# A hybrid decoder layer on one core: a new hand order for TensorE's mixer work

## The chip, the core and the metric

The kernel runs on one core of a Trainium2 chip. A core has five engines with an instruction queue each: TensorE (PE in the profile; its weight loads are listed as PEld), VectorE (DVE), ScalarE (ACT), GpSimd (POOL) and SyncE (SP), which here only starts transfers. The metric is the device time of one execution in microseconds; less is better.

## What is computed

One layer of a decoder, for 1024 prompt tokens and 8 sequences of 8 new tokens each, 1088 tokens in all, in 32-bit floats:

```python
x = x + 0.5 * rms(swiglu(rms(x) @ w_up1) @ w_down1)
h = rms(x); z = h @ w_in                  # q,k,v | qkv of B | z | a,b | gates
oA = sliding_window_attention(q, k, v)    # window 128, 8 heads, 2 kv heads, a sink per head
q, k, v = silu(conv4(qkv))                # short causal convolution, branch B
oB = gated_delta_rule(l2(q), l2(k), v, decay, beta)   # 4 heads, chunks, state 128x128
oB = rms(oB) * silu(z)
m = sigmoid(gA) * (oA @ w_a) + sigmoid(gB) * (oB @ w_b)
x = x + rms(m @ w_out)
x = x + 0.5 * rms(swiglu(rms(x) @ w_up2) @ w_down2)
```

Caches and states for the next call are outputs too.

## The kernel before

Features lie on the partitions and tokens along the free axis, in three chunks `CH` of 384, 384 and 320 tokens (the last holds 256 prompt tokens and the 64 new ones). The three stages follow each other: feed-forward 1, the mixers, feed-forward 2. A projection of the mixers is cut into units of 128 output features. `gemm` (L142 to L144) multiplies in three products for each of 8 slices of the input features: high part by high part, high by low part of the activations, low part of the weights by high. One slice of one chunk, so three products, is called a **k-step** here. Weights arrive raw, ScalarE copies out the high part (L115) and VectorE subtracts it for the low part (L116).

In the mixers the program order of TensorE is the order in which the code is written (`manual_schedule`). The other engines' orders are the scheduler's, by priorities; each engine then runs its rows strictly in that order. Between the small products of the attention and of the delta rule the code calls `fill(us)`: it takes k-steps from the front of `queue`, a list of generators, until their planned costs (0.54 us for 384 tokens, 0.46 us for 320) reach the number given. The queue's units are

- `z_unit` and `gate_unit`: the projections for z and for the gates gA and gB, 24 k-steps each. A gate's result needs little of VectorE: ScalarE's tanh, and one L672 on VectorE in the last chunk;
- `conv_unit`: a projection of branch B, followed on VectorE by three multiply-adds (L865) and by L893 a chunk, with a tail for the new tokens in the last chunk (L875, L885 to L890).

The attention runs over 16 items. `att_s` makes the scores (L954), VectorE adds the mask (L965) and does the softmax (L815 to L818, L822 to L824), and one item later `att_t` transposes what L824 wrote (L983); `att_v` (L999) is one more item behind. A fill stands after each item.

The delta rule takes the heads in two pairs. For a pair, `first` makes the products of keys and queries (L1192, read by VectorE's L1195, and L1202, read by L1205), `invert` solves 32x32 triangles on VectorE over a transfer out and back, with one long fill for TensorE meanwhile, and `second` (from L1255 on) combines the blocks, runs the decode over 8 chunks (L1315, L1323, L1333, L1342, L1343), multiplies the state of the new tokens (L1355: 16 columns a product), and ends with the norm products (L1395). `together(a, b)` alternates two heads at each `yield`; a yield's two numbers are the fill after the first head's piece and after the second's. The results of these products use two PSUM tiles `ph` and two `py`; the queue's units use three tiles `pa`, and the heads share one tile `po` for L1333.

What is left of the queue after the second pair is done by `finish`, then come the last two gates, and then `br`, the branch products, whose inputs are loaded (L1505) and split (L195 on ScalarE, L196 on VectorE) from what the mixers wrote to memory.

Of the kernel before, what the change touches and what calls it, by code (L numbers as in the profile page):

```python
# [13 lines left out]
P = 128  # L14
# [21 lines left out]
def body(ctx: ExitStack, tc: tile.TileContext, d):  # L36
# [769 lines left out]
    def st():  # L806
        return s2b.tile([P, 20], F32, tag="st", name=uid("st"), bufs=4)
# [27 lines left out]
    def fill(us):  # L835
        while us > 0 and queue:
# [3 lines left out]
            else:  # L840
                us -= t

    def finish(units):
        for u in units:
            if u in queue:
                queue.remove(u)
                drain(u)
# [100 lines left out]
    def att_s(it):  # L948
        n, tp2 = items[it]
        k0 = 128 if n == 0 else 0  # L950
        ps = (ph(), py())
        for j in range(2):
            for g2, hs in enumerate(half2):
                mm = nc.tensor.matmul(  # L954
                    ps[g2][:, j * 256 + k0 : j * 256 + 256],
                    YA[tp2 * 2 + j][hs, n * P : n * P + P],
                    kT[hs, (n - 1) * P + k0 : (n + 1) * P],
                    start=True,
                    stop=True,
                )  # L960
                if masked:
                    tc.add_manual_dep(mm.ins, masked[-1], SYNC, reason="both halves start together")
        s4 = sbs[it % 2][:, :1024].rearrange("p (h k) -> p h k", k=256)[:, :, k0:256]
        for g2 in range(2):
            mask = nc.vector.tensor_tensor(  # L965
                out=s4[:, 2 * g2 : 2 * g2 + 2, :],
                in0=ps[g2].rearrange("p (j k) -> p j k", k=256)[:, :, k0:256],
                in1=cst[:, C_AM + k0 : C_AM + 256].unsqueeze(1).to_broadcast([P, 2, 256 - k0]),
                op=ALU.add,
            )  # L970
        masked.append(mask.ins.name)
        softmax(s4, vec[:, V_SK + 4 * tp2 : V_SK + 4 * tp2 + 4], st())

    def att_t(it):
        n, tp2 = items[it]
# [35 lines left out]
    def attention_prompt():  # L1011
        n = len(items)
        for it in range(n + 2):
            if it < n:
                att_s(it)
            if it >= 2:
                att_v(it - 2)
            if 1 <= it <= n:
                att_t(it - 1)
            fill(7.5 if it == 0 else 8.5 if it == n - 1 else 4.8)  # L1020
        for t in range(4):
            nc.sync.dma_start(oad[t, :, :NPR], YA[t][:, :NPR])

# [78 lines left out]
    class Head:  # L1102
# [140 lines left out]
        def second(self, pks):  # L1243
# [75 lines left out]
            for c in range(8):  # L1319
                w, cs, ix = chunk_of(c, h)  # L1320
                p = ps[c]
                if c > 0:
                    nc.tensor.matmul(p[:, 0:128], M[:, cs], S, start=False, stop=True)  # L1323
                vns = ar[:, c % 2, :]
                nc.vector.tensor_scalar_mul(vns, p[:, 0:128], tk["kds"][:, ix : ix + 1])
                vn = ar[:, 2 + c % 2, :]
                nc.scalar.copy(vn, p[:, 0:128])
                yield 0.0, 0.0
                if c < 7:
                    uv(c + 1)  # L1330
                yield 0.0, 0.4
                pk = pks()[:, 128 * (h % 2) : 128 * (h % 2) + 128]
                nc.tensor.matmul(pk, k[:, cs], vns, start=True, stop=True)  # L1333
                S2 = ar[:, 4 + c % 2, :]
                if c > 0:
                    nc.vector.scalar_tensor_tensor(
                        out=S2, in0=S, scalar=tk["gtot"][:, ix : ix + 1], in1=pk, op0=ALU.mult, op1=ALU.add
                    )
                else:
                    nc.vector.tensor_copy(S2, pk)  # L1340
                if c > 0:
                    nc.tensor.matmul(p[:, 256:384], S, q[:, cs], start=True, stop=False)  # L1342
                nc.tensor.matmul(p[:, 256:384], vn, QK[:, cs], start=c == 0, stop=True)  # L1343
                nc.scalar.copy(QK[:, cs], p[:, 256:384])
                S = S2
                yield 0.0, 0.0
            nc.sync.dma_start(d["dpo"][h], S)

            ss = slice(NPR, NT)
# [3 lines left out]
            mqv = mq.rearrange("p (g b t) -> p b g t", g=2, t=8)  # L1353
            for b in range(8):
                nc.tensor.matmul(pv[:, b], S0[:, b, :], mqv[:, b], start=b == 0, stop=False)  # L1355
            nc.tensor.matmul(p[:, 0:64], v8, U[:NSM, ss], start=False, stop=True)
            vnT = ar[:, 0, 0:64]
            nc.scalar.copy(ar[:, 0, :], p[:, 0:128])
# [29 lines left out]
                    out=L[:, 512 * hf : 512 * hf + 512], in0=L[:, 512 * hf : 512 * hf + 512], in1=p6, op=ALU.add  # L1388
                )
            nc.sync.dma_start(d["dso"][:, h].rearrange("b p e -> p b e"), S0)  # L1390
            yield 0.0, 5.0
            for a, b in CH:
                cs = slice(a, b)
                pq = pb()
# [9 lines left out]
    def together(a, b):  # L1404

        for us in a:
            fill(us[0])
            fill(next(b)[1])

    def invert(heads):  # L1410

        a, b = heads
        Md, Ld = (t[:68, :NPR].rearrange("p (r s) -> p r s", s=32) for t in (a.A[7], b.A[7]))
        tt = a.R2
        for i, x in enumerate(heads):
            nc.sync.dma_start(Md[34 * i : 34 * i + 34], bm[x.h])
        nc.vector.memset(Ld, 0.0)
        nc.vector.memset(b.A[7][:68, 0:1024:33], 1.0)
        for j in range(31):
            m = 31 - j  # L1420
            tv = tt[:68, : m * (j + 1)].rearrange("p (a b) -> p a b", b=j + 1)
            nc.vector.tensor_tensor(
                out=tv,
                in0=Md[:, j + 1 :, j : j + 1].to_broadcast([68, m, j + 1]),
                in1=Ld[:, j : j + 1, 0 : j + 1].to_broadcast([68, m, j + 1]),
                op=ALU.mult,
            )
            nc.vector.tensor_tensor(out=Ld[:, j + 1 :, 0 : j + 1], in0=Ld[:, j + 1 :, 0 : j + 1], in1=tv, op=ALU.subtract)
        nc.vector.tensor_copy(Md, Ld.rearrange("p r s -> p s r"))
        for i, x in enumerate(heads):  # L1430
            h, L, U = x.h, x.A[1], x.A[5]
            nc.sync.dma_start(blocks32(ud[h]), Md[34 * i : 34 * i + 32])
            nc.sync.dma_start(bu[h][32:34], Md[34 * i + 32 : 34 * i + 34])
            nc.sync.dma_start(blocks32(ld[h]), Ld[34 * i : 34 * i + 32])
            nc.sync.dma_start(U[:, :NPR].rearrange("p (c s) -> p c s", s=P), whole_rows(ud[h]))
            nc.sync.dma_start(L[:, :NPR].rearrange("p (c s) -> p c s", s=P), whole_rows(ld[h]))
            for b2 in range(2):
                nc.sync.dma_start(U[32 * b2 : 32 * b2 + 32, NPR + 32 * b2 : NPR + 32 * b2 + 32], bu[h][32 + b2])
        fill(51.0)

    heads = [Head(h, (HA, YA)[h % 2]) for h in range(4)]
    zs = [z_unit(h) for h in range(4)]
    gates = [gate_unit(i) for i in range(14)]
    with tc.manual_schedule(engines={mybir.EngineType.PE}):
        queue += zs[0:2] + gates[0:3] + heads[0].conv
        fill(2.0)
        values()
        attention_prompt()
# [3 lines left out]
        for hs in (heads[0:2], heads[2:4]):  # L1452
# [10 lines left out]
            else:  # L1463
# [7 lines left out]
                b.keys()  # L1471
                drain(b.conv[2])
                queue += zs[2:4] + gates[10:14]
            together(a.first(), b.first())
            invert(hs)
            state = []
# [211 lines left out]
```

## Time and profile before

| | before |
|---|---|
| median of 3 runs | 2410.01 us (2409.04 to 2410.94) |
| profiled execution | 2409.66 us |
| its span | 2407.7 us |
| mean granted TensorE clock | 0.990 |
| TensorE busy | 2354.6 us, 98% |
| VectorE busy | 1698.4 us, 71% |
| ScalarE busy | 1111.5 us, 46% |

The span runs from the first to the last instruction; 1.96 us of the profiled execution lie around it. A granted clock of 1.00 is 2.4 GHz, 0.50 is 1.2 GHz. "Busy" counts the time in which an instruction of the engine was running, at whichever clock.

### The profile page before, as it was taken

To read this page: it belongs to the slowest core of one execution; us is meant where nothing else is said; L and a number is where in the kernel's file an instruction comes from. 1 tells how busy PE (TensorE), PEld (TensorE's weight loads), DVE (VectorE), ACT (ScalarE), POOL (GpSimd) and SP (SyncE) were. 2 spreads that over 40 slices of the span, in tenths; PEclk is the share of its full clock that TensorE was granted. 3 is DMA by queue.
4 is the path that set the end of the run, shared out by engine and by line. 5 is a ranking of instruction groups with operands and counts; after the bars stand their busy time and mean duration, and the time that the engine had idled before them with its cause. 6 is when DMAs were issued, how large, how long until landed. Compare 5 with 4: busy or idle time off the path is not lost. (4 is left out here: it accounts for less than half of the span.)

```text
span 2407.7 us, 38879 instructions
## 1 busy us (share of the span) xinstructions
PE 2354.6 (98%) x14535; PEld 2295.2 (95%) x14535; DVE 1698.4 (71%) x3453; ACT 1111.5 (46%) x2314; POOL 22.1 (1%) x21
## 2 busy tenths in 40 slices
PE   8999999999999999999999999999999999999997
PEld 8999999999998988899898989999999999999997
DVE  8887667667688667675497457588976567676677
ACT  7644424323365455552563453366644433333344
POOL 0000000000000000000000000000000000000000
PEclk9999999999999999999999999999999999999998
DMA  7332212212453521314322346456433222122453
GB/s 274 120 121 86 67 51 84 71 58 91 167 191 130 181 69 48 126 45 125 105 98 70 99 153 203 131 195 221 134 104 94 67 62 79 62 71 84 158 168 130
DMA packets 173828, 276.19 MB, mean 115 GB/s; under 512 B 35276, under 2 KB 76208, under 8 KB 173632
## 3 DMA queue, kind: packets, MB, share of 16 engines
q1 hardware_dynamic: 173640, 273.71, 35.5%
q8 instruction: 114, 1.87, 0.3%
q14 instruction: 74, 0.61, 0.1%
HBM read 231.22 MB, written 43.41 MB: 114 GB/s over the span
## 5 line engine op out<-in xcount | busy, mean ns | idle before, releaser
L466 PE MATMUL pa<-ch,h_c_s 128*128 128x384 f32 x704 | 236.6, 336 | 3.1 <-DVE t L472 2.6
L468 PE MATMUL pa<-ch,l_c_s 128*128 128x384 f32 x704 | 235.6, 335 | 0.0
L467 PE MATMUL pa<-cl,h_c_s 128*128 128x384 f32 x704 | 235.5, 334 | 0.0
L472 DVE TENSOR_TENSOR t<-pa,t 128x384 f32<-128x384 f32 x308 | 170.6, 555 | 87.1 <-PE pa L468 87.0
L466 PE MATMUL pa<-ch,h_c_a 128*128 128x384 f32 x528 | 177.1, 335 | 0.0
L468 PE MATMUL pa<-ch,l_c_a 128*128 128x384 f32 x528 | 176.9, 335 | 0.0
L467 PE MATMUL pa<-cl,h_c_a 128*128 128x384 f32 x528 | 176.8, 335 | 0.0
L115 ACT CAST h_c_a<-r_c_a 128x512 fp32r<-128x512 f32 x132 | 81.8, 620 | 128.9 <-PE pa L467 111.9
L466 PEld LDWEIGHTS pa<-ch,h_c_s 128*128 128x128 f32 x704 | 132.2, 188 | 6.4 <-DVE t L472 6.3
L467 PEld LDWEIGHTS pa<-cl,h_c_s 128*128 128x128 f32 x704 | 132.2, 188 | 0.0
L468 PEld LDWEIGHTS pa<-ch,l_c_s 128*128 128x128 f32 x704 | 132.2, 188 | 0.0
L115 ACT CAST h_c_s<-q_c_s 128x512 fp32r<-128x512 f32 x132 | 82.0, 622 | 105.6 <-PE pa L467 92.4
L142 PE MATMUL pa<-xbh,h_ga 128*128 128x384 f32 (+1 forms) x384 | 130.8, 341 | 0.0
L144 PE MATMUL pa<-xbh,l_ga 128*128 128x384 f32 (+1 forms) x384 | 127.0, 331 | 0.0
L143 PE MATMUL pa<-xbl,h_ga 128*128 128x384 f32 (+1 forms) x384 | 127.0, 331 | 0.0
L466 PEld LDWEIGHTS pa<-ch,h_c_a 128*128 128x128 f32 x528 | 99.2, 188 | 0.4 <-ACT t L384 0.2
L468 PEld LDWEIGHTS pa<-ch,l_c_a 128*128 128x128 f32 x528 | 99.2, 188 | 0.0
L467 PEld LDWEIGHTS pa<-cl,h_c_a 128*128 128x128 f32 x528 | 99.2, 188 | 0.0
L115 ACT CAST h_c_s<-r_c_s 128x512 fp32r<-128x512 f32 x44 | 27.4, 622 | 149.5 <-PE pa L467 120.4
L142 PE MATMUL pa<-xbh,h_qkv 128*128 128x384 f32 (+1 forms) x288 | 95.5, 332 | 0.0
L144 PE MATMUL pa<-xbh,l_qkv 128*128 128x384 f32 (+1 forms) x288 | 94.3, 327 | 0.0
L143 PE MATMUL pa<-xbl,h_qkv 128*128 128x384 f32 (+1 forms) x288 | 94.2, 327 | 0.0
(627 smaller groups left out, 7277.8 us busy)
## 6 DMA issues: line engine op xcount, KB each, us to landing
r_c_a<-in_up_dram SPq DMA_DIRECT2D x132, 256.0 KB
r_wo<-in_wo_dram SPq DMA_DIRECT2D x48, 256.0 KB
q_c_a<-in_up_dram SPq DMA_DIRECT2D x44, 256.0 KB
q_ub<-in_up_dram SPq DMA_DIRECT2D x44, 256.0 KB
r_ub<-in_up_dram SPq DMA_DIRECT2D x44, 256.0 KB
r_ua<-in_up_dram SPq DMA_DIRECT2D x42, 256.0 KB
q_ua<-in_up_dram SPq DMA_DIRECT2D x42, 256.0 KB
r_da<-in_dn_dram SPq DMA_DIRECT2D x40, 256.0 KB
```

The costliest lines, as they stand in the source:

```text
L115: nc.scalar.copy(hi, full)
L142: nc.tensor.matmul(ps[:, :n], hi[:, j, :], at(xh, k), start=first, stop=False)
L143: nc.tensor.matmul(ps[:, :n], hi[:, j, :], at(xl, k), start=False, stop=False)
L144: mm = nc.tensor.matmul(ps[:, :n], lo[:, j, :], at(xh, k), start=False, stop=last)
L466: nc.tensor.matmul(ps, wh[:, k, :], xh[:, k, :], start=k == 0, stop=False)
L467: nc.tensor.matmul(ps, wh[:, k, :], xl[:, k, :], start=False, stop=False)
L468: nc.tensor.matmul(ps, wl[:, k, :], xh[:, k, :], start=False, stop=k == 3)
L472: nc.vector.tensor_tensor(out=out, in0=ps, in1=other, op=ALU.add)
```

## The change

It writes TensorE's work in the mixers in another order and gives some of VectorE's rows another priority. No product is added or taken away.

1. `turns` alternates the first head's three convolutions with the first three gates, chunk by chunk. Before, the three gates came first and the convolutions behind them.
2. The mask and the softmax of an attention item get a higher priority on VectorE and ScalarE.
3. The fill after the last attention item grows from 8.5 to 9.5.
4. A fill of 5.0 stands ahead of `first`.
5. `invert`'s fill grows from 51.0 to 53.5 for the second pair.
6. In the decode the k-step after the second head's L1315 (one each of the 8 chunks) goes; in the odd chunks one stands between the two heads' L1333 instead.
7. The 8 pairs of L1355's products are cut in two halves, with a k-step after each head's first half.
8. The fill ahead of the norm products shrinks from 5.0 to 2.0 for the first pair.

```diff
+    def turns(us, vs):
+
+        for pair_ in zip(us, vs):
+            for _ in CH:
+                for u in pair_:
+                    for _ in range(KT):
+                        yield next(u)
+            for u in pair_:
+                drain(u)
+
...
-        for g2 in range(2):
-            mask = nc.vector.tensor_tensor(
...
-        masked.append(mask.ins.name)
-        softmax(s4, vec[:, V_SK + 4 * tp2 : V_SK + 4 * tp2 + 4], st())
+        with tc.high_priority(offset=10000):
+            for g2 in range(2):
+                mask = nc.vector.tensor_tensor(
...
+            masked.append(mask.ins.name)
+            softmax(s4, vec[:, V_SK + 4 * tp2 : V_SK + 4 * tp2 + 4], st())
...
-            fill(7.5 if it == 0 else 8.5 if it == n - 1 else 4.8)
+            fill(7.5 if it == 0 else 9.5 if it == n - 1 else 4.8)
...
                 if c < 7:
                     uv(c + 1)
-                yield 0.0, 0.4
+                yield 0.0, 0.0
                 pk = pks()[:, 128 * (h % 2) : 128 * (h % 2) + 128]
                 nc.tensor.matmul(pk, k[:, cs], vns, start=True, stop=True)
...
                 S = S2
-                yield 0.0, 0.0
+                yield 0.4 * (c % 2), 0.0
...
             for b in range(8):
                 nc.tensor.matmul(pv[:, b], S0[:, b, :], mqv[:, b], start=b == 0, stop=False)
+                if b == 3:
+                    yield 0.4, 0.4
...
-            yield 0.0, 5.0
+            yield 0.0, 5.0 if h > 1 else 2.0
...
-        fill(51.0)
+        fill(51.0 if a.h == 0 else 53.5)
...
-        queue += zs[0:2] + gates[0:3] + heads[0].conv
+        queue += zs[0:2] + [turns(heads[0].conv, gates[0:3])]
...
+            fill(5.0)
             together(a.first(), b.first())
```

Lines of the changed kernel stand some 10 to 14 lines further down, so L824 keeps its number, but L954 becomes L964, L1192 becomes L1203, L1355 becomes L1366 and so on.

VectorE's order around the tail of the first convolution (`t` are the convolution's buffers, `s` the scores, `st` the softmax's small vectors, `pa` the PSUM tiles of the queue's units). Before:

```order
L885 TENSOR_SCALAR t_851_10310<-t_850_10306,vec 128x64
L865 SCALAR_TENSOR_TENSOR t_851_10310<-t_850_10306,vec,t_851_10310 128x256
L887 TENSOR_SCALAR t_852_10315<-t_850_10306,vec 128x64
L889 COPY sn_10318<-ncv 128x3
L890 COPY sn_10318<-t_850_10306 128x24
L888 TENSOR_TENSOR t_851_10310<-t_851_10310,t_852_10315 128x64
L965 TENSOR_TENSOR s_8347<-ph_10355,cst 128x512
L822 TENSOR_TENSOR st_10236<-st_10236 128x4
L887 TENSOR_SCALAR t_852_10315<-t_850_10306,vec 128x64
L823 RECIPROCAL st_10236<-st_10236 128x4
L965 TENSOR_TENSOR s_8347<-py_10356,cst 128x512
L824 TENSOR_TENSOR s_8355<-s_8355,st_10236 128x1024
```

and of the change, at the first convolution's tail:

```order
L898 TENSOR_TENSOR t_811_9913<-t_811_9913,t_812_9918 128x64
L897 TENSOR_SCALAR t_812_9918<-t_810_9909,vec 128x64
L898 TENSOR_TENSOR t_811_9913<-t_811_9913,t_812_9918 128x64
L897 TENSOR_SCALAR t_812_9918<-t_810_9909,vec 128x64
L116 TENSOR_TENSOR l_ga_0_10452<-r_ga_0_10449,h_ga_0_10451 128x512
L822 TENSOR_TENSOR st_9845<-st_9845 128x4
L898 TENSOR_TENSOR t_811_9913<-t_811_9913,t_812_9918 128x64
L823 RECIPROCAL st_9845<-st_9845 128x4
L875 SCALAR_TENSOR_TENSOR t_811_9913<-t_810_9909,vec,t_811_9913 128x256
L672 SCALAR_TENSOR_TENSOR t_815_9936<-pa_9884,r_8287 128x320
L116 TENSOR_TENSOR l_ga_1_10458<-r_ga_1_10455,h_ga_1_10457 128x512
L824 TENSOR_TENSOR s_8347<-s_8347,st_9845 128x1024
```

The next item's mask (L965) no longer stands ahead of L824 there; a gate's L672, which needs the gate's finished tile `pa_9884`, and one weight split L116 now do.

TensorE's order at the start of the first pair's `first` (`qkv` and `ga` are weights of a convolution and of a gate; `eye` is the identity for transposes). Before:

```order
L142 MATMUL pa_11466<-xbh_1_8284,h_qkv_1_11388 128x320
L143 MATMUL pa_11466<-xbl_1_8286,h_qkv_1_11388 128x320
L144 MATMUL pa_11466<-xbh_1_8284,l_qkv_1_11389 128x320
L1192 MATMUL ph_11520<-s_8348,s_8349 128x128 x4
L1194 MATMUL py_11521<-eye_72,s_8355 128x128 x4
L1192 MATMUL ph_11534<-s_8342,s_8343 128x128 x4
L1194 MATMUL py_11535<-eye_72,s_8347 128x128 x4
L1192 MATMUL ph_11546<-s_8348,s_8349 128x128 x4
```

and of the change:

```order
L142 MATMUL pa_11533<-xbh_1_8284,h_ga_1_10909 128x320
L143 MATMUL pa_11533<-xbl_1_8286,h_ga_1_10909 128x320
L144 MATMUL pa_11533<-xbh_1_8284,l_ga_1_10910 128x320
L1203 MATMUL ph_11557<-s_8348,s_8349 128x128 x4
L1205 MATMUL py_11558<-eye_72,s_8355 128x128 x4
L1203 MATMUL ph_11571<-s_8342,s_8343 128x128 x4
L1205 MATMUL py_11572<-eye_72,s_8347 128x128 x4
L1203 MATMUL ph_11583<-s_8348,s_8349 128x128 x4
```

The last convolution's k-steps no longer stand right ahead of the products: 11 k-steps of a gate do (4 of 384 tokens, 7 of 320). For the second pair there are 10 k-steps of z, of 384 tokens.

TensorE's order from the last decode chunk to the state products (head a writes `ph`, head b `py`). Before:

```order
L142 MATMUL pa_12402<-xbh_1_7322,h_ga_1_12398 128x384
L143 MATMUL pa_12402<-xbl_1_7324,h_ga_1_12398 128x384
L144 MATMUL pa_12402<-xbh_1_7322,l_ga_1_12399 128x384
L1333 MATMUL po_12546<-s_8355,s_8352 128x128
L1342 MATMUL ph_12519<-s_8348,s_8355 128x128
L1343 MATMUL ph_12519<-s_8354,s_8355 128x128
L1333 MATMUL po_12546<-s_8347,s_8340 128x128
L1342 MATMUL py_12521<-s_8342,s_8347 128x128
L1343 MATMUL py_12521<-s_8346,s_8347 128x128
L1355 MATMUL ph_12558<-mq_10996,s_8349 128x2x8 x8
L1356 MATMUL ph_12558<-s_8353,v_10998 128x64
```

and of the change:

```order
L1354 MATMUL ph_12544<-s_8354,s_8355 128x128
L142 MATMUL pa_12367<-xbh_1_7900,h_ga_1_12193 128x384
L143 MATMUL pa_12367<-xbl_1_7902,h_ga_1_12193 128x384
L144 MATMUL pa_12367<-xbh_1_7900,l_ga_1_12194 128x384
L1344 MATMUL po_12565<-s_8347,s_8340 128x128
L1353 MATMUL py_12546<-s_8342,s_8347 128x128
L1354 MATMUL py_12546<-s_8346,s_8347 128x128
L1366 MATMUL ph_12580<-mq_10996,s_8349 128x2x8 x4
L142 MATMUL pa_12367<-xbh_1_7900,h_ga_1_12193 128x384
L143 MATMUL pa_12367<-xbl_1_7902,h_ga_1_12193 128x384
L144 MATMUL pa_12367<-xbh_1_7900,l_ga_1_12194 128x384
L1366 MATMUL py_12589<-mq_11017,s_8343 128x2x8 x4
```

In this odd chunk the k-step has moved from ahead of head a's products to between the two heads' products, and a new one stands inside the state products. In even chunks there is none.

## Rows read from the trace of the kernel before

**Rows 1.** The page's first part: busy time of each engine, share of the span.

```profile
PE 2354.6 (98%) x14535; PEld 2295.2 (95%) x14535; DVE 1698.4 (71%) x3453; ACT 1111.5 (46%) x2314; POOL 22.1 (1%) x21
```

**Rows 2.** Waits of TensorE, 840 to 1460 us: us in total, times, longest.

```profile
PE ph L1192 <- DVE s L1195: 8.2, 2, 4.5
PE ph L983 <- DVE t L888: 3.1, 1, 3.1
PE ph L1255 <- DMA s<-ud: 2.1, 1, 2.1
PE pa L142 <- DVE t L1518: 1.4, 1, 1.4
...
PE po L1333 <- DVE s L1340: 0.5, 2, 0.3
```

**Rows 3.** Windows: length, busy time of each engine, TensorE's granted clock, DMA share, GB/s.

```profile
966.00:972.00 6.00, 4.42 (x21) 4.45 (x22) 3.78 (x11) 3.03 (x11) 0.00 (x0) 0.72 0.00 0
1065.00:1074.00 9.00, 7.09 (x38) 7.10 (x39) 7.56 (x22) 2.81 (x5) 0.00 (x0) 0.62 0.02 4
1181.00:1187.00 6.00, 6.00 (x27) 5.47 (x27) 3.00 (x6) 0.74 (x3) 1.90 (x1) 0.72 0.48 166
1277.00:1286.00 9.00, 6.10 (x35) 6.10 (x36) 8.22 (x22) 3.33 (x6) 0.00 (x0) 0.62 0.22 62
1392.00:1402.00 10.00, 10.00 (x52) 9.62 (x52) 2.82 (x7) 2.06 (x6) 3.79 (x2) 0.66 0.47 139
1406.00:1412.00 6.00, 5.44 (x19) 4.45 (x19) 2.43 (x5) 0.47 (x1) 0.00 (x0) 0.72 0.62 175
1156.00:1176.00 20.00, 20.00 (x151) 18.71 (x151) 9.06 (x28) 8.72 (x31) 0.00 (x0) 1.00 0.23 75
```

**Rows 4.** VectorE's timeline, 958 to 968: start, us, line and operation.

```profile
961.64 0.42 DVE L672 SCALAR_TENSOR_TENSOR t<-pa,r 128x256 f32<-128x256 f32 x1
961.98 0.68 DVE L116 TENSOR_TENSOR l_ga<-r_ga,h_ga 128x512 fp32r<-128x512 f32 x1
...
966.22 1.22 DVE L824 TENSOR_TENSOR s<-s,st 128x1024 f32<-128x1024 f32 x1
```

**Rows 5.** TensorE's timeline, 962 to 969.

```profile
962.29 0.48 PE L954 MATMUL ph<-s,s 64*128 64x256 f32 x1
...
963.35 1.08 PE L999 MATMUL po<-s,s 128*64 128x256 f32 x8
```

**Rows 6.** VectorE's timeline, 1061 to 1083.

```profile
1066.16 0.69 DVE L1195 TENSOR_TENSOR s<-ph,s 128x512 f32<-128x512 f32 x1
...
1071.58 0.69 DVE L1195 TENSOR_TENSOR s<-ph,R 128x512 f32<-128x512 f32 x1 [0.70 <-PE ph L1192]
...
1073.60 1.13 DVE L1205 SCALAR_TENSOR_TENSOR s<-ph,nk,s 128x128 f32<-128x128 f32 x4 [0.74 <-PE ph L1202]
```

**Rows 7.** TensorE's timeline, 1060 to 1082.

```profile
1060.32 1.05 PE L1192 MATMUL ph<-s,s 128*128 128x128 f32 x8
...
1080.67 0.42 PE L142 MATMUL pa<-xbh,h_ga 128*128 128x384 f32 x1
```

**Rows 8.** TensorE's timeline in the decode, one chunk from L1342 on.

```profile
1157.32 0.39 PE L1342 MATMUL ph<-s,s 128*128 128x128 f32 x2
1157.54 0.39 PE L1343 MATMUL ph<-s,s 128*128 128x128 f32 x2
1157.92 0.49 PE L1333 MATMUL po<-s,s 128*128 128x128 f32 x2
...
1160.98 0.49 PE L1333 MATMUL po<-s,s 128*128 128x128 f32 x2
```

**Rows 9.** TensorE's timeline: the last chunk of the last gates, then the branch products.

```profile
1441.19 0.31 PE L142 MATMUL pa<-xbh,h_ga 128*128 128x320 f32 x1
...
1448.22 0.34 PE L142 MATMUL pa<-oabh,h_br 128*128 128x384 f32 x1
```

**Rows 10.** VectorE's timeline: the last split of the branches' inputs.

```profile
1457.72 0.49 DVE L196 TENSOR_TENSOR oabl<-o,oabh 128x320 fp32r<-128x320 f32 x1 [0.88 <-ACT oabh L195]
```

More of the change, by code (lines that the diff above doesn't have):

```diff
@@ L963, in att_s @@
         s4 = sbs[it % 2][:, :1024].rearrange("p (h k) -> p h k", k=256)[:, :, k0:256]
-        for g2 in range(2):
-            mask = nc.vector.tensor_tensor(
[L966 to L970, printed above, removed]
-        masked.append(mask.ins.name)
-        softmax(s4, vec[:, V_SK + 4 * tp2 : V_SK + 4 * tp2 + 4], st())
+        with tc.high_priority(offset=10000):
+            for g2 in range(2):
+                mask = nc.vector.tensor_tensor(
+                    out=s4[:, 2 * g2 : 2 * g2 + 2, :],
+                    in0=ps[g2].rearrange("p (j k) -> p j k", k=256)[:, :, k0:256],
+                    in1=cst[:, C_AM + k0 : C_AM + 256].unsqueeze(1).to_broadcast([P, 2, 256 - k0]),
+                    op=ALU.add,
+                )
+            masked.append(mask.ins.name)
+            softmax(s4, vec[:, V_SK + 4 * tp2 : V_SK + 4 * tp2 + 4], st())
     def att_t(it):
```

## The prediction

> **What bounds the kernel now.** I read the page's busy shares first. TensorE is busy for 2354.6 us of a span of 2407.7, the next engine for 71% [rows 1]. No product goes away, so the change can only win time in which TensorE stood still, some 53 us in the whole kernel, or ran at the lower clock. The second view is the list of TensorE's waits in the mixers [rows 2]; the reader sees that a handful of places hold nearly all of it, and that four of the five are waits for VectorE. The third view is windows around these places, read for the granted clock [rows 3]: a mean of 0.72 over 6 us says that half the speed was missing for 3.4 us, so that work worth (1 - 0.72) x 6 = 1.7 us at 2.4 GHz was not done. By this rule the six places lose 1.7, 3.4, 1.7, 3.4, 3.4 and 1.7 us. The last view is the timelines of VectorE and TensorE at each place, for who is late there.
>
> I call the places A (the attention, 966), B (`first` of pair 0, 1066), C (its L1355, 1182), E and G, H (`first`, L1355 and L1386 of pair 1, 1278, 1394 and 1407) and F (L1255 of pair 1).
>
> **Part by part.**
>
> *A: turns and the softmax's priority.* L983 waits 3.1 us [rows 2] for L824, which VectorE begins only at 966.22, ends 1.22 us later [rows 4], and before which it works off the convolution's tail (the first order listing). The clock falls behind it and costs 1.7 [rows 3]. Together 4.8. With conv and gate in turn, VectorE's load is spread, and the softmax has priority over the multiply-adds. What replaces the wait is in the second listing: L824 now stands behind a gate's L672 and a split L116, and L672 needs the chunk's last k-step. From there VectorE needs 0.4 (L672 of 320), 0.6 and 1.2 [rows 4], 2.2 us and some handing over. TensorE meanwhile has the scores and `att_v`, from 962.29 to 963.35 + 1.08 = 964.43, 2.1 us [rows 5]. So 0.1 to 0.5 is left open, I take 0.35, and there are two such places in the new order: 0.7. Sum **-4.1**; the bounds are -4.8 and, if the wait stays and only moves, 0.
>
> *B: 5.0 of fill ahead of `first`, pair 0.* TensorE issues its first products at 1060.32 and is through at 1080.67 [rows 7], and in between it stood still for 3.7 us (8.2 less the other pair's 4.5) [rows 2], since L1195 cannot start before 1066.16 [rows 6]: VectorE is in the last convolution's rows until then. The fill is 4 k-steps of 384 tokens and 7 of 320. A k-step of 320 takes 0.44 us (16 of them, 48 products, between the first and the last row of [rows 9], 7.03 us); one of 384 by that 0.53. So 5.2 us of work from the queue now lie where TensorE waited, and the products begin at 1065.5, when VectorE is about to be free. The pace inside `first` is VectorE's. There it waited twice for products at the lower clock, 0.70 and 0.74 us [rows 6]; with the idle gone I expect these waits gone too, so that the end comes 1.3 us earlier. The work of the fill would have been done later in any case: 5.2 + 1.3 = 6.5, less 0.1 for the handing over, **-6.4**. Bounds: if the waits stay, -5.2; if the clock falls all the same and the fill's end runs at half, -4.
>
> *E: the same for pair 1.* The wait is 4.5 us [rows 2], the fill 10 k-steps of 384, 5.2 us. VectorE's order has one more row (0.5 us) of a z unit ahead of L1195 and two of the tail ahead of the third, so I expect only 0.5 of an earlier end: **-5.7**. Bounds -6.4 and -3.
>
> *F: 53.5 instead of 51.0.* L1255 waits 2.1 us for the load of `ud` [rows 2]. Five more k-steps delay TensorE by some 2.3 us against the chain of VectorE and SP, which starts with `first`'s end as before; the same transfers stand ahead in SP's queue. The wait is filled: **-2.1**. If the chain comes 1 us later against TensorE, -1. Pair 0 has no such wait, and its fill stays.
>
> *Decode.* A chunk takes 3.06 us (from L1333 of b to the next, [rows 8]). Between L1342 and L1343 lie 0.22 us, between L1343 and b's L1333 0.38: b waits 0.16 for the tile `po`, until VectorE has read a's product. In the four odd chunks the k-step now stands there and covers it: 0.17 x 4 = 0.7 a pair. In the even chunks no k-step is left between L1323 and a's L1333. VectorE has to scale a's result there; the second head's L1323 and the two L1315 cover it by about 0.15 us, which I read from the same timeline, so I cost it at nothing. If the cover failed by 0.2 it would be 0.8 a pair, the whole gain. The wait in the first chunk, 0.5 for both pairs [rows 2], is nearly covered too, 0.4. Sum **-1.8**, bounds -1.9 and 0.
>
> *C, G, H: pieces in L1355.* TensorE was busy all through C and G, 6.00 of 6.00 and 10.00 of 10.00 us, and still the clock fell [rows 3]: products of 16 columns stood there. With a k-step in the middle of each head's products the spell of thin products is halved; but the decode ahead of it has four k-steps less. No row shows which of the two decides. Nothing to 6.8 us is to be won; I take a third, **-2.2**, since only two k-steps come in where four go just ahead.
>
> *Where the work is missing later.* The queue runs dry sooner. In pair 0 one k-step is left between L1386 and the norm products instead of ten; their inputs were long done there, so I cost it at nothing (if one is late: up to 4 us). After pair 1 twelve k-steps are missing ahead of the last gates, so the branch products start 5.7 us sooner against the chain that feeds them (norm, transfer out and in, splits). Its last split starts at 1457.72 [rows 10], 9.5 us after the first product [rows 9], but that one is for the last chunk. Today TensorE waits 1.4 us [rows 2] for L1518, which stands on VectorE behind these splits; in the new order the rows that read the branch products (L1531, L1532, the former L1517, L1518) stand ahead of more of them. I take **0**, between -1.4 and +5.7.
>
> **Sum.** -4.1 - 6.4 - 5.7 - 2.1 - 1.8 - 2.2 = -22.3. The profiled execution took 2409.66 us (span and 1.96 around it), so 2387.4; the median of the runs lies 0.35 higher, so 2387.7, **2388 us**.
>
> **Rivals.**
>
> *The clock falls all the same (2397).* In `first` one long wait becomes many short ones on the two `ph` and two `py` tiles that VectorE must empty. Then A gives back 1.7, C, G, H give nothing (2.2), B and E lose their earlier ends (1.3 + 0.5) and half of their fills runs at half speed (3.4): 9.1 us, 2397. For it: C and G fell without any idle. Against: in B the clock came back during just such products, as the mean of 0.62 over 9 us says (a spell of 6.8 us). The Trainium skill (TensorE: Matmul & The Clock Gate, section "A second HAM failure mode: psum-queue depth-cycling") tells of a kernel in which frequent micro-idles between groups, from cycling through PSUM, made the clock swing between its two levels; by that rule this rival is the likelier one and the time 2397. The trace so far bears it out only in part, by the recovery just named.
>
> *Given back where the filler is gone (2394).* The branch products wait for their splits: +5.7, or the norm products do: +4. For it: the DMA engines and VectorE are loaded there, and the wait of 1.4 exists already. Against: the first chunk's tiles are needed first and loaded first.
>
> *VectorE is the bound in `first` (2400).* The fill's own splits and L672 push L1195 back as far as TensorE is later: B and E give nothing, -10.2 in all. Against: in VectorE's new order only one split and one z row stand ahead.
>
> *Slower: the decode runs at the lower clock (2406 to 2424).* It loses four of eight k-steps a pair, and its products are of 128 columns and fewer. At half speed the 2.2 us of products of a chunk cost up to 2.2 more; 8 chunks make 18 us a pair, so 2406 with one pair and 2424 with both. It decides from ten slow chunks on (22 us). Against: in 1156 to 1176, decode throughout, the clock is 1.00 and TensorE busy for 20.00 of 20.00 us [rows 3].
>
> **How the numbers follow.** Forecast 0.54, the clock 0.20, given back 0.14, VectorE 0.06, the decode 0.06. The range takes in the forecast, with the bounds that help (C, G, H whole and B, E, A at their best: -31, 2379), the second and third and most of the fourth: 2379 to 2402. The forecast's own range is 2381 to 2394. By 0.2% (4.8 us), about what a measurement of this kernel can tell from no change, faster is all but the decode and a little of the rest, 0.90; same 0.04; slower 0.06.
>
> **What would show it.** A: no wait over 0.5 us at L994 (the former L983). B and E: no wait at L1203 over 1 us, and a gate's or z's k-steps right ahead. F: no wait at the former L1255. Decode: 2.5 us in even chunks, 2.9 in odd ones. C, G, H: granted clock near 1.00 around the state products. The branch products: waits at L142 for L1531 and L1532 of 1 to 2 us. Wrong it would be if VectorE's softmax still ends late in the attention, if the clock is at 0.50 in new places, or if the waits at the branch products grow by over 4 us.

## The result and the profile after

| | before | change |
|---|---|---|
| median of the runs, us | 2409.53 (2408.81 to 2410.94) | 2394.01 (2392.79 to 2400.75) |
| profiled execution, us | 2409.66 | 2392.79 |
| ratio to before, 95% interval | 1 | 0.994 (0.9928 to 0.9951) |

The change is 0.6% faster: 15.5 us by the medians, 16.9 by the two profiled executions (the change's is the fastest of its four). Forecast were 2388 and a range of 2379 to 2402.

The page's first part of the change, which answers to [rows 1]:

```profile
PE 2344.9 (98%) x14535; PEld 2286.1 (96%) x14535; DVE 1697.5 (71%) x3453; ACT 1112.6 (47%) x2314; POOL 21.0 (1%) x21
```

The instruction counts are equal, so nothing but standing still and the lower clock can have gone. TensorE's waits in the mixers, from 830 to 1460 us (in total, times, longest), against [rows 2]:

```profile
PE ph L994 <- DVE s L824: 5.3, 6, 1.8
PE pa L142 <- DVE t L1532: 3.1, 2, 2.2
PE py L1408 <- ACT s L1409: 0.9, 1, 0.9
...
PE ph L1312 <- ACT s L1313: 0.8, 1, 0.8
PE py L1399 <- DVE s L1400: 0.4, 1, 0.4
PE po L1344 <- DVE s L1336: 0.4, 2, 0.2
PE ph L1203 <- DVE s L1206: 0.3, 1, 0.3
```

`first` has shrunk from 8.2 us to 0.3, the wait for `ud` has left the list, and two rows have grown: the attention's wait for the softmax (5.3 in six places) and the branch products' wait for L1532 (3.1). Windows of the change at four places of the argument (columns as in [rows 3]):

```profile
1063.00:1081.00 18.00, 17.38 (x139) 16.14 (x138) 16.94 (x52) 7.69 (x18) 1.54 (x1) 1.00 0.26 68
1275.00:1293.00 18.00, 17.33 (x129) 16.15 (x130) 11.72 (x33) 7.10 (x16) 4.80 (x2) 1.00 0.24 58
1380.00:1400.00 20.00, 19.82 (x98) 16.48 (x98) 9.61 (x22) 3.63 (x12) 3.79 (x2) 0.83 0.38 128
1440.00:1450.00 10.00, 7.78 (x36) 7.46 (x35) 7.21 (x16) 3.47 (x8) 0.00 (x0) 0.83 0.89 284
```

Both `first` now run at 1.00 throughout. The half speed that is left in the mixers and branches stands around pair 1's state products (0.83 over 20 us, 3.4 us) and, new, in the branch products (0.83 over 10 us, 1.7).

For each execution with a profile I added up, over windows of 10 us, what TensorE stood still (length less busy time) and what it lost to the lower clock ((1 - granted clock) x length). The attention is 850 to 1000 us, pair 0 goes on to 1210, pair 1 to 1420, the branches to 1480, and the last column to 2370; what lies ahead of 850 and behind 2370 is left out. Both kernels and seven of the experiments below, standing still / lost to the clock, us:

| kernel | attention | pair 0 | pair 1 | branches | behind, to 2370 |
|---|---|---|---|---|---|
| before | 4.0 / 1.7 | 5.0 / 5.1 | 8.4 / 8.5 | 1.7 / 0 | 4.1 / 1.7 |
| change | 5.5 / 0 | 2.1 / 0 | 2.1 / 3.4 | 3.1 / 1.7 | 2.4 / 0 |
| turns_without_priority | 6.3 / 0 | 2.1 / 1.7 | 2.5 / 3.4 | 3.3 / 1.7 | 3.6 / 1.7 |
| priority_without_turns | 1.5 / 0 | 1.4 / 3.4 | 1.9 / 1.7 | 3.7 / 1.7 | 1.4 / 0 |
| convolutions_last | 0.9 / 0 | 2.9 / 8.5 | 1.8 / 3.4 | 2.7 / 0 | 4.8 / 3.4 |
| old_decode_steps | 5.5 / 0 | 1.5 / 8.5 | 2.7 / 5.1 | 3.0 / 1.7 | 3.6 / 1.7 |
| no_fill_before_first | 5.5 / 0 | 5.3 / 3.4 | 4.6 / 3.4 | 2.9 / 1.7 | 4.7 / 1.7 |
| short_norm_fill_both_pairs | 5.5 / 0 | 1.8 / 5.1 | 2.4 / 1.7 | 4.2 / 0 | 5.0 / 1.7 |
| priority_and_late_inputs | 1.6 / 0 | 1.4 / 5.1 | 2.0 / 1.7 | 1.8 / 1.7 | 3.7 / 0 |

The gain is in the two pairs; the attention as a whole gave nothing. Behind the branch products' start the two kernels take the same 959.5 us: what the branches lost, the part behind them (whose code is the same) won back, among it a spell of half speed that only the execution before had there. That part is chance: with the same code the last column lies between 1.4 us in all (priority_without_turns) and 8.2 (convolutions_last).

### The profile page after: what moved, and what is told of

Same layout as the page of the kernel before. It is cut to its first block, busy times and chain, and to the rows that moved or that the text cites. A ratio compares the mean times of both kernels' runs of the same rounds, so it can differ in the third digit from the quotient of the medians.

```text
span 2390.9 us, 38846 instructions
## 1 busy us (share of the span) xinstructions
PE 2344.9 (98%) x14535; PEld 2286.1 (96%) x14535; DVE 1697.5 (71%) x3453; ACT 1112.6 (47%) x2314; POOL 21.0 (1%) x21
```

## Experiments

All edits are relative to the change; ratios are to the kernel before on the same chip, as is the change's own 0.994.

**Attention: turns or priority?** Two kernels, each with one half.

```diff
-        with tc.high_priority(offset=10000):
...
+            softmax(s4, vec[:, V_SK + 4 * tp2 : V_SK + 4 * tp2 + 4], st())
```

(turns_without_priority; mask and softmax stay as in the kernel before)

> The change with the softmax and mask at their old priority; the turns and all else stay. Theory 1 (the priority rows make VectorE run one item's normalisation L824 ahead of the next item's mask, so each softmax starts late and TensorE waits at L994 in several items): the waits at L994 fall from 5.3 us to under 2, no stall of over 2 us, and the time is 2390 to 2392. Rival (the priority is what keeps the convolution's rows out of the softmax's way; what is left are the convolution's and splits' rows): waits at L994 of over 5 us, one of them with a fall of the clock, time 2394 to 2399.

```diff
-        queue += zs[0:2] + [turns(heads[0].conv, gates[0:3])]
+        queue += zs[0:2] + gates[0:3] + heads[0].conv
```

> The change with the three gates ahead of the three convolutions again, as before the change; the softmax's priority and all else stay. Theory 1 (the turns are the useful half of the attention's edits): the waits move to the convolutions, from 940 us on, 3 to 6 us in all, with a fall of the clock, time 2395 to 2399. Rival (the priority alone takes the long stall away, since L824 stands ahead of the convolution's tail): waits at L994 under 4 us, clock 1.00 in the attention, time 2390 to 2393.

With turns alone 2397.09 (ratio 0.9948, 0.9934 to 0.9961), and the attention's idle stays, at 6.3, as the rival had it (but with no fall of the clock). With the priority alone 2389.57 (0.9920, 0.9908 to 0.9932), 0.0020 x 2410 = 4.8 us better than the change by the two ratios, whose intervals overlap by a little (4.4 by the medians, from two chips); the attention's idle falls to 1.5. The wait in priority_without_turns:

```profile
PE ph L994 <- DVE s L824: 1.3, 2, 0.7
```

So the priority is the useful half and the turns cost some 4 us.

**Is L824 late because splits and L672 stand ahead of it?** The prediction had it so.

```diff
-        with tc.high_priority(offset=10000):
+        with tc.high_priority(offset=30000):
```

> The change with the offset 30000 for mask and softmax instead of 10000, so that L824 stands ahead of the weight splits L116 and of a gate's L672 on VectorE. Theory 1 (the waits at L994 come from the order mask behind L824 and from ScalarE's exponentials, so this changes little): waits at L994 4 to 5.5 us, time 2392 to 2395. Rival (L116 and L672 ahead of L824 are the cost): the waits of 1.8 and 0.6 us at the convolutions' tails go, waits at L994 2.5 to 3.5, time 2390 to 2392; if splits come late, L142 waits for them.

2395.92 (0.9942, 0.9929 to 0.9954), above both ranges. The wait at L994 falls from 5.3 to 3.9, between the two. At the change's longest wait the rows that the prediction had named do stand ahead of L824. VectorE, and with the last row TensorE:

```profile
924.82 0.46 DVE L875 SCALAR_TENSOR_TENSOR t<-t,vec,t 128x256 f32<-128x256 f32 x1
925.19 0.48 DVE L672 SCALAR_TENSOR_TENSOR t<-pa,r 128x320 f32<-128x320 f32 x1
925.59 0.68 DVE L116 TENSOR_TENSOR l_ga<-r_ga,h_ga 128x512 fp32r<-128x512 f32 x1
926.19 1.22 DVE L824 TENSOR_TENSOR s<-s,st 128x1024 f32<-128x1024 f32 x1
...
927.56 0.63 PE L994 MATMUL ph<-eye,s 128*128 128x128 f32 x4 [1.79 <-DVE s L824]
```

With the offset 30000 this wait is gone, but two of 1.6 stand an item later, where the convolution's L875 and L902 come between the maximum and the exponentials. So the splits are a part and not the main cause. The change has such a wait too, of 0.76 at 943.98. VectorE ahead of it:

```profile
936.78 1.21 DVE L815 TENSOR_REDUCE st<-s 128x4 f32<-128x1024 f32 x1
937.91 0.61 DVE L875 SCALAR_TENSOR_TENSOR t<-t,vec,t 128x384 f32<-128x384 f32 x1
...
939.16 0.16 DVE L818 TENSOR_SCALAR st<-st 128x4 f32<-128x4 f32 x1
...
942.20 0.16 DVE L822 TENSOR_TENSOR st<-st 128x4 f32<-128x4 f32 x1 [1.80 <-ACT s L821]
942.61 1.22 DVE L824 TENSOR_TENSOR s<-s,st 128x1024 f32<-128x1024 f32 x1
```

and ScalarE, same kernel:

```profile
939.20 0.53 ACT L902 ACTIVATE t<-t 128x384 f32<-128x384 f32 x1 [2.09 <-DVE t L875]
939.73 0.49 ACT L821 ACTIVATE s<-s,st 128x256 f32<-128x256 f32 x1
```

Mask, maximum (L815), the small rows L816 to L818, exponentials (L821), scaling (L824) and the next item's mask are one chain. The maximum is done at 938.0. But on VectorE L816 to L818 stand among two L875 and are done only at 939.3, and on ScalarE the exponentials stand behind the convolution's L902, which waits 2.09 us for L875 and begins at 939.20. From the end of the maximum to the first exponential that is 1.7 us, against 0.5 in an item without convolution rows (879.59 to 880.13). VectorE in turn waits 1.80 us for the exponentials. The turns put convolution chunks under the softmax all along; in the old order gates come first.

**Then convolutions after the attention should free it.**

```diff
-        queue += zs[0:2] + [turns(heads[0].conv, gates[0:3])]
+        queue += zs[0:2] + gates[0:5] + heads[0].conv
...
-        finish(list(queue))
-        queue += gates[3:5]
         attention_sample()
+        finish(list(queue))
```

> The change with five gates ahead of the first head's convolutions in the attention's queue instead of turns; the convolutions' k-steps then fill the new tokens' attention, which comes before the rest of them is drained. Theory (VectorE and ScalarE rows of a convolution chunk, three multiply-adds between the mask and the maximum and a tanh ahead of the exponentials, stretch the serial softmax chain beyond TensorE's time for an item; turns put twice as many convolution chunks under the softmax): the waits at L994 in the items fall to about 1 us, the attention loses 4 us less than in the change; pair 0 has 11 k-steps less of filler, so some wait at the norm products; time 2388 to 2392. Rival (any alternation of units costs, whatever their VectorE rows, since weight splits come due): waits at L994 of 4 us and more, time 2393 to 2397.

The wait, which answers to the first row of the change's list:

```profile
PE ph L994 <- DVE s L824: 0.6, 1, 0.6
```

The account of the attention holds: idle 0.9 for 5.5. The time is not better and far outside the forecast, 2398.77 (0.9950, 0.9937 to 0.9962): pair 0, which has 11 k-steps less, lost 8.5 us to the clock and waited 1.2 at L1399.

**A smaller move of the same kind**, which leaves pair 0 its work:

```diff
-        queue += zs[0:2] + [turns(heads[0].conv, gates[0:3])]
+        queue += zs[0:2] + gates[0:4] + heads[0].conv
...
-        finish(list(queue))
-        queue += gates[3:5]
         attention_sample()
+        finish(list(queue))
...
-                queue += gates[5:10]
+                queue += gates[4:10]
```

> The change with four gates ahead of the first head's convolutions, which then fill the last attention items and the new tokens' attention; one gate more is left for pair 0, whose queue then reaches beyond its norm products. Theory (few convolution rows under the softmax, and filler among the thin products of both pairs): idle in the attention 1 to 2 us instead of 5.5, no wait at the norm products of pair 0, less half clock around 1180 than in the run with five gates; time 2385 to 2390, faster than the change by 4 us or more. Rival (the clock around the state products falls by chance whatever the filler): 2390 to 2395.

2402.22 (0.9961, 0.9948 to 0.9974), 12 us or more above the forecast. The attention's idle is 0.9 again, but now two products of the new tokens' attention (L1061) wait for the L824 of its own softmax. The three longest waits:

```profile
PE pa L142 <- DVE t L1531: 3.2, 1, 3.2
PE py L1061 <- DVE s L824: 2.4, 1, 2.4
PE ph L1061 <- DVE s L824: 2.4, 1, 2.4
```

and its window there:

```profile
1000.00:1030.00 30.00, 25.20 (x196) 22.04 (x195) 22.72 (x104) 14.27 (x43) 0.88 (x2) 0.77 0.37 125
```

The wait has moved, and it has the clock fall besides (0.23 x 30 = 6.9 us). That convolutions stand beside this attention is not enough to make it wait: they do in convolutions_last too, and there it does not. Here the queue, one gate shorter, runs dry. The last k-step ends at 1010.7, so 7.3 us after the scores TensorE is at L1061 (1003.46 to 1010.74, no k-step until 1023.91); in convolutions_last the fill of 13.0 is done in full (1000.91 to 1013.92).

**`first`: the fill.**

```diff
-            fill(5.0)
             together(a.first(), b.first())
```

> The change without the fill of 5.0 ahead of the first products; all else stays. Theory (this fill is the main gain: 5.2 us of work in place of 3.8 and 4.4 us of idle, and the clock's falls behind these go): the waits at L1203 for L1206 come back with 3 to 4 us each and the clock falls behind each (3.4 us a pair); 10 to 11 k-steps a pair come later, which takes away the waits at the norm and branch products (up to 4 us); time 2400 to 2405. Rival (the turns alone move the convolution's rows away, so VectorE is free earlier anyway): waits at L1203 under 1.5 us, time within 3 us of the change's.

2407.29 (0.9984, 0.9974 to 0.9994), so the fill of both pairs is worth 0.0044 x 2410 = 10.6 us by the ratios (13.3 by the medians). The profiled executions give less. The two `first` take 18.05 and 17.11 us here (1064.87 to 1082.92, 1271.88 to 1288.99) and 13.48 and 14.06 in the change, so 7.6 more; from the attention's first scores to the first branch product it is 10.0 more, and the other 4.4 of the 14.4 between these executions lie outside of this stretch. So some 8 to 10 us, half of the whole gain or more, are the fill's. Without it

```profile
PE ph L1203 <- DVE s L1206: 6.9, 2, 3.8
```

stands again. This time the clock did not fall behind these two waits; the half speed stood elsewhere, so the fall at `first` need not follow from the wait.

**Decode: the k-steps' old places.**

```diff
-                yield 0.0, 0.0
+                yield 0.0, 0.4
...
-                yield 0.4 * (c % 2), 0.0
+                yield 0.0, 0.0
```

> The change with the decode's k-steps where they stood before (one after the second head's L1326 in each chunk); the halves of L1366 and all else stay. Theory (the removed k-step covered the copy and the scaling of a chunk's result; the new order gives back what it saves, 0.3 us a pair is left of 0.9): the decode's pair takes 4 k-steps more, which the queue then lacks later; time 2393 to 2396, so 0 to 2 us more. Rival (the decode's new places are worth the 1.8 us that were forecast or more, since they also keep the filler of L1366 available): 2396 to 2398.

2396.87 (0.9962, 0.9946 to 0.9979): inconclusive. It is 2.9 us above the change by the medians, while the runs differ by 13 among themselves (2393.07 to 2406.14), and the two intervals overlap. TensorE's timelines tell more. One row of before, which stands ahead of those of [rows 8], and two chunks of the change:

```profile
1157.10 0.38 PE L1333 MATMUL po<-s,s 128*128 128x128 f32 x2
```

```profile
1159.42 0.49 PE L1344 MATMUL po<-s,s 128*128 128x128 f32 x2
...
1161.12 0.39 PE L1344 MATMUL po<-s,s 128*128 128x128 f32 x2
1161.42 0.49 PE L1353 MATMUL ph<-s,s 128*128 128x128 f32 x2
1161.75 0.39 PE L1354 MATMUL ph<-s,s 128*128 128x128 f32 x2
...
1162.50 0.38 PE L1344 MATMUL po<-s,s 128*128 128x128 f32 x2
...
1164.92 0.49 PE L1344 MATMUL po<-s,s 128*128 128x128 f32 x2
```

An odd chunk takes 1162.50 - 1159.42 = 3.08, an even one 2.42, together 5.50 with one k-step, against 2 x 3.06 = 6.12 with two [rows 8]. A k-step of 384 is some 0.53, so 0.09 us are won, where 0.17 were forecast for the odd chunk. All chunks together give still less: from b's first L1344 to its last a pair takes 19.21 and 19.19 us with 4 k-steps, and before 20.85 with 7 (pair 0) and 20.70 with 7, two of them of 320 tokens (pair 1). Less the k-steps, 0.05 and 0.10 us a pair are won. The removed k-step had been covering something: in the odd chunks, too, none stands ahead of a's products any more, and a's L1344 to L1353 and L1353 to L1354 are now 0.30 and 0.33, before 0.22 each (1157.10, 1157.32, 1157.54).

**State products: pieces.**

```diff
-                if b == 3:
-                    yield 0.4, 0.4
```

> The change without the k-step inside L1366's products. Theory (the filler among the thin products keeps the clock up in most executions): granted clock 0.50 after L1366 in both pairs in most executions, time 2394 to 2398. Rival (the clock there falls by chance of where the thin products lie, filler or not): times spread as the change's do, median within 2 us of it, 2392 to 2396.

```diff
-                if b == 3:
+                if b in (1, 3, 5):
```

> The change with L1366's eight pairs of products cut in four pieces of two, a k-step after each of the first three for each head. Theory (share of thin products decides about the clock): no stretch at 0.50 after L1366 in either pair, time 2388 to 2392, small spread. Rival (chance, or the decode steps ahead decide): the clock still falls in one of the pairs, time 2392 to 2396.

Without pieces 2401.09 (0.9967, 0.9954 to 0.9979), above both ranges, and not by the clock at the state products, which was 1.00 in pair 1 and cost 5.1 in pair 0. The largest new loss is one wait, `oabh`'s at the branch products:

```profile
PE pa L142 <- ACT oabh L195: 5.4, 1, 5.4
```

ScalarE:

```profile
1418.36 1.28 ACT L1408 ACT_TABLE_LOAD   x1
1419.66 0.53 ACT L1408 ACTIVATE s<-s 128x384 f32<-128x384 f32 x1
1420.20 1.28 ACT L931 ACT_TABLE_LOAD   x1
...
1439.15 0.51 ACT L195 CAST oabh<-o 128x384 fp32r<-128x384 f32 x1 [3.69 <-DMA o<-oad]
```

The root of the norm (here L1408, in the change L1410) and the last gates' tanh (L931) alternate, and each turn loads a function table: ten loads from 1390 to 1450, against six in the change. Four more are 4 x 1.28 = 5.1 us, about the wait, but that they make it is not shown. L195 itself waits 3.69 us for its transfer. SyncE issues that at 1434.55, in the change at 1421.38: it stands in SyncE's queue behind the gates' stores (L932), which wait for the tanh, and behind loads of weights (L130), which wait for VectorE's splits. short_norm_fill_both_pairs has eight table loads and no wait for `oabh`.

With three pieces 2398.28 (0.9949, 0.9935 to 0.9963), again above both ranges. Its windows at the two pairs' state products:

```profile
1180.00:1200.00 20.00, 18.76 (x65) 11.53 (x64) 9.93 (x20) 7.66 (x17) 4.20 (x2) 0.74 0.49 153
...
1380.00:1400.00 20.00, 19.82 (x143) 19.20 (x144) 7.36 (x21) 6.26 (x22) 3.75 (x2) 1.00 0.36 113
```

One pair is low, the other whole, with the same pieces in both, and without pieces it was the same way round; in the change it was the other way. So pieces alone don't decide the clock there.

**Norm: the short fill in both pairs.**

```diff
-            yield 0.0, 5.0 if h > 1 else 2.0
+            yield 0.0, 2.0
```

> The change with a fill of 2.0 ahead of the norm products for the second pair too, so that some 7 k-steps come behind the norm products and the branch products start 3 us later against the chain that feeds them. Theory (the branch products' waits of 3.1 us and the clock's fall behind them come from too little filler between norm and branch): waits at L142 for L1532 under 1 us, no 0.50 at 1445, a wait of up to 1 us at the norm products of pair 1, time 2389 to 2392. Rival (VectorE's splits are the bound there, and their loads start no earlier): waits of 2 us and more stay, time 2393 to 2395.

2398.31 (0.9950, 0.9937 to 0.9963), above both ranges; the waits at the branch products stay, as the rival had it (2.0 for L1532, 1.1 for L1531, 1.2 for a split). More k-steps ahead of them don't help. VectorE in the change shows what stands in the way:

```profile
1434.39 3.83 DVE L196 TENSOR_TENSOR oabl<-o,oabh 128x384 fp32r<-128x384 f32 x8
1438.14 0.55 DVE L1532 SCALAR_TENSOR_TENSOR t<-t,pa 128x384 f32<-128x384 f32 x1
...
1441.34 1.48 DVE L196 TENSOR_TENSOR oabl<-o,oabh 128x320 fp32r<-128x320 f32 x3 [0.56 <-ACT oabh L195]
1442.73 0.55 DVE L1532 SCALAR_TENSOR_TENSOR t<-t,pa 128x384 f32<-128x384 f32 x1
```

L1532 reads the first chunk's products and frees TensorE's tile. Its first row stands behind eight splits of 384 tokens; its second, for which TensorE waits 2.2 us, stands behind the third chunk's (320 tokens), of which one waits for ScalarE.

**So the third chunk's load and splits go behind the first chunk's products.**

```diff
+    def inputs(c):
+        a, b = CH[c]
...
+    for c in range(2):
+        inputs(c)
...
+            if q4 == 0 and c == 0:
+                inputs(2)
```

On top of four_gates_then_convolutions, then on top of priority_without_turns:

> The run before with one thing more: the third chunk's branch inputs are loaded and split after the first chunk's branch products in program order, so that VectorE's rows that read the first branch products no longer stand behind the third chunk's splits. Theory (TensorE's waits for L1531 and L1532 come from these splits standing ahead on VectorE, not from too little filler): waits at L142 at the branch products under 1.5 us instead of about 3, no clock fall behind them, 2 to 4 us less than the run before. Rival (the inputs of the first chunk come too late in any order): the waits stay.

> The best parts together: the change without the turns (three gates, then the convolutions, as before the change), with the softmax's priority, and with the third chunk's branch inputs loaded and split after the first chunk's branch products. Theory (the two effects lie in different stages and add): idle in the attention 1.5 us, waits for the branch products' VectorE rows under 1 us with no clock fall behind them, 2 to 4 us less than the run with the priority alone, so 2385 to 2389. Rival (chance falls of the clock around the state products cover it): 2389 to 2394.

The first: 2399.26 (0.9955, 0.9941 to 0.9969), 3.0 less than without the late inputs by the medians (the intervals overlap), and in the place of 3.2 us

```profile
PE pa L142 <- DVE t L1534: 0.6, 2, 0.3
```

The second: 2391.47 (2382.92 to 2394.52), ratio 0.9905 (0.9888 to 0.9922), the lowest of all. Its interval lies wholly below the change's; it overlaps that of priority_without_turns, so what the late inputs add there is not settled. Waits at the branches: 1.4 for a split and 0.3 for `oabh`; the clock cost 1.7 there all the same.

## Why the prediction was right, and where it was not

From the attention's first scores (853.86; before 852.59) to the first branch product (1431.44; 1448.22 [rows 9]) the change is 18.0 us shorter. Its terms, as measured in the profiled executions:

| place | forecast | measured |
|---|---|---|
| A | -4.1 | -0.2 |
| B | -6.4 | -6.9 |
| E | -5.7 | -6.3 |
| F | -2.1 | -1.3 |
| decode | -1.8 | -0.2 |
| C, G, H | -2.2 | -3.4 |
| norm | 0 | +0.9 |
| branches | 0 | +3.1, won back behind them |

The measured ones make -17.4 up to the branch products, the forecast ones -22.3. Two small waits that the table does not list went as well (L1395 of pair 1, 0.5, and 0.4 of L1386's 0.8), which makes -18.3 for the -18.0. The attention began 1.3 later, where nothing was changed, and 959.5 us follow in both. That is the 16.9. One sum of the prediction does not come out: the best bounds of its parts add up to -28.4 and not to -31, so the lower end of the range would have been 2382.

**A failed, and it is the largest part of the miss.** The step "With conv and gate in turn, VectorE's load is spread" took VectorE's load for the limit. The limit is a chain through two engines, and the turns made it late in five places, not the two that I had counted (the sixth wait in the list, 0.62 at 886.00, was there before, at 884.74). At the longest one, a place that I had priced at 0.35, the sum let VectorE begin L672 as soon as the gate's last k-step was done, at 923.2. VectorE was in the convolution's tail until 925.19, and the wait was 1.79. The clock did come back, as forecast (1.7 won), and the new waits ate it (1.5 more idle). That the turns cost this is shown by priority_without_turns (1.5 of idle) and convolutions_last (0.9). The sign that I had named, no wait over 0.5 at L994, did not come. Of the three signs of being wrong two came: the softmax still ends late, and the clock is at 0.50 in a new place (1440 to 1450); the waits at the branch products grew by 1.4, not by over 4.

**B and E held, and somewhat more.** TensorE's timeline of the change at `first`, against [rows 7]:

```profile
1067.01 1.05 PE L1203 MATMUL ph<-s,s 128*128 128x128 f32 x8
...
1080.49 0.39 PE L142 MATMUL pa<-xbh,h_ga 128*128 128x320 f32 x1
...
1271.83 1.05 PE L1203 MATMUL ph<-s,s 128*128 128x128 f32 x8
...
1285.89 0.42 PE L142 MATMUL pa<-xbh,h_z 128*128 128x384 f32 x1
```

and pair 1 before:

```profile
1272.63 1.05 PE L1192 MATMUL ph<-s,s 128*128 128x128 f32 x8
...
1293.01 0.42 PE L142 MATMUL pa<-xbh,h_z 128*128 128x384 f32 x1
```

13.48 and 14.06 us, against 20.35 and 20.38. The rival in which VectorE is the bound fell with it: L1203 waits 0.3. But not all of it is the fill's. In no_fill_before_first the two `first` are 18.05 and 17.11, so 2.3 and 3.3 us less than before without any fill, with the clock at 1.00. The fill brings 4.6 and 3.1 where I had put 5.2 each; that the sums held all the same, because the clock stayed up there with and without the fill, is partly luck.

**The decode** ran at full clock in both pairs (pair 0 lost nothing, pair 1 only from its state products on), so the rival on the other side of no change fell. Its term was mis-sized, -1.8 against -0.2: I looked for a lost cover in the even chunks alone, but the odd ones lost theirs too, and the first chunks' waits, of which I had counted 0.4 as won, are still 0.4 of 0.5 (L1344). **F:** the wait for `ud` is gone (2.1), but 0.8 at L1312 for ScalarE is new.

**C, G, H** gave more than the third I had taken, but by chance: pair 0's TensorE order is the same in the change, turns_without_priority and short_norm_fill_both_pairs, and its loss to the clock was 0, 1.7 and 5.1. The size that one execution shows here is no measure of an edit; in its place a spread of some 5 us belonged in the range.

**Branches:** +3.1, of it 1.4 of idle and 1.7 of clock, from L1532 behind the second and third chunks' splits. My reason for 0, that the rows which read the branch products stand ahead of more of the splits, held for too few of them. So the rival "given back where the filler is gone" was there with about half of its price, and that 3.1 were won back behind it is chance. That the median is this rival's 2394 is chance too: what made the difference from 2388 is mostly A and the decode.

**The rival of the clock** (many short waits instead of one long): the granted clock of the change is 1.00 over the attention, six waits of 5.3 us in all included:

```profile
850.00:1000.00 150.00, 144.51 (x957) 1.00 0.20 65
```

and 1.00 over both `first` (the windows above). The Trainium skill (TensorE: Matmul & The Clock Gate, section "A second HAM failure mode: psum-queue depth-cycling") tells of frequent micro-idles that made the clock swing; here it did not swing where they are.

**What stays open:** what makes the spells at half speed, which cost 1.7 us or a multiple of it, come and go with the same order of products. The runs show only where they stand, and that the pieces alone don't decide it. Edits 3, 5 and 8 were not taken out one at a time, so F and the norm products rest on the timelines alone.

## What to carry to other kernels

Filler ahead of a stage that another engine is not yet ready for is worth most of its length, if it is taken from where TensorE is not waiting: 7.6 of 10.4 us inside the two `first`, and half or more of the gain. Before work is spread under a chain that crosses two in-order engines, list what lands ahead of each link on both: two multiply-adds on VectorE and a tanh on ScalarE made one link 1.2 us later, while VectorE then stood idle for 1.80. Where runs differ by spells of the clock, read the idle in the place that was changed, and leave gains of 1 or 2 us to that reading.

## What the runs showed of the hardware that I had not expected

The clock fell with TensorE busy throughout. A window of short_norm_fill_both_pairs (same order there as in the change):

```profile
1020.00:1040.00 20.00, 20.00 (x133) 0.91 0.17 48
```

and of the change:

```profile
1020.00:1040.00 20.00, 20.00 (x141) 1.00 0.19 57
```

A table load on ScalarE takes 1.28 us each time that tanh and root alternate. The Trainium skill (ScalarE activation tables: per-element evaluation and per-set limits, section "What a function is on this engine") puts two functions of different sets one load of 1283 ns apart; the trace agrees.
